# NSA attention operands of 64 and 15 partitions zero-padded to 128, and the first weight slab on ScalarE's queue

## The chip, the cores and the metric

The kernel runs on one core of a Trainium2 chip. The metric is the device time of one execution in microseconds (us), the median of several runs. In the profile PE is TensorE's matmul, PEld its weight load, DVE is VectorE, ACT ScalarE, POOL GpSimd, SP SyncE; SPq is the queue of SyncE that issues DMAs.

## The reference

One hybrid decoder layer on x of 256 tokens and 2048 columns, batch 1, all in float32:

```
xn = rms(x, norm_attn)
fq, fk, fv, f_logit, nq, kc, vc, ks, vs, kw, vw, nsa_gate, gate_a, gate_b = split(xn @ w_in)
o_a = fox_attention(...)                    # 8 heads of 128, causal, with forget gates
o_b = nsa_attention(...)                    # 8 heads, q and k of 192, v of 128, 2 key groups
h = x + (sigmoid(gate_a) * (o_a @ w_up_fox) + sigmoid(gate_b) * (o_b @ w_up_nsa)) @ w_out
y = h + (silu(rms(h) @ w_ffn_gate) * (rms(h) @ w_ffn_up)) @ w_ffn_down
```

The NSA branch adds three attentions under per-head gates: over 15 compressed keys and values (a small MLP over blocks of 32 tokens), over selected blocks, and over a window. With 256 tokens the selection takes every block.

## The kernel before

The kernel is a stream of weight slabs. A `Chunk` is a slab of up to 128 x 1024 float32 weights (two blocks of 128 rows by 512 columns). `load` (L151) issues its DMA from SyncE's queue into one of five `raw` buffers; `split` (L156) makes two parts of it for fp32r matmuls, `hi` on ScalarE (L160) and `lo = raw - hi` on VectorE (L161), four buffers each; `gemm` multiplies them in three passes (L183 high by high, L184 high by low, L185 low by high) for two token tiles of 128, into the PSUM tiles `acc`. The last loop of the program drives the stream: it loads up to eight slabs ahead, splits up to three ahead, issues the matmuls of a slab, and after each calls `slot`, which lets waiting tasks (generators: norms, transposes, attention) go one step on. So the order on every engine is fixed when the program is built, and the attention's matmuls stand between slabs of the weight stream.

At the start of the program SyncE's queue issues `vna` (the gains of the first norm, L119), then the first 512 columns of x for both token tiles (L97), the first two slabs of 512 columns (L153), the next x, and so on. Twelve transposes of the identity (L235) run on TensorE meanwhile. ScalarE starts with a warm activation (L123) that loads its table. VectorE copies the transposed `vna` to `vecT` (L238), clears one column of each key tile (L403), and goes on with the first `lo` (L161) and the low parts of the transposed x (L261).

`nsa_attention` is such a task, and treats eight heads, each in three steps. The score step (L740 to L766) has three blocks of keys of 272, 256 and 272 columns. The 192 columns of a head's q and k are kept as 128 and 64. The first 128 take three passes (L752 to L754). The other 64 are kept twice on 128 partitions: `qb` has the high part of q on partitions 0 to 63 and its low part on 64 to 127, `kbh` the high part of k on both halves, so that L755 does two passes in one matmul. The third pass is L756, high part of q by low part of k, on 64 partitions:

```
nc.tensor.matmul(o, qb[:, h, q], kbh[:, g, k], start=False, stop=False)
nc.tensor.matmul(o, qb[:64, h, q], kbl[:, g, k], start=False, stop=True)
```

`softmax_parts` makes the probabilities on VectorE and ScalarE (L641 to L650). The next step transposes them (L726 to L732) and writes them to `ph`, `pl` and `p1` (L733 to L737); the 15 compressed keys take columns 512 to 767 of `ph` and `pl`, on 15 partitions. The value step (L712 to L716) runs three passes each with `vhl` twice and with `vcg`, the 15 compressed values, on 15 partitions, and then two float32 matmuls with `vsw` (L715, L716), all into one PSUM tile. `put_k` (L375) writes the key tiles, `cmp_finish` (L539) writes `vcg`.

Of the kernel before, what the change touches and what calls it, by code (L numbers as in the profile page):

```python
# [14 lines left out]
P = 128  # L15
# [17 lines left out]
class Chunk:  # L33
    """A slab of weight rows that is loaded, split and multiplied as one unit."""

# [18 lines left out]
def hybrid_block(ctx: ExitStack, tc: tile.TileContext, x, norm_attn, w_in, fox_f_bias,  # L54
# [30 lines left out]
    def wk(shape, tag, bufs, dt=F32):  # L85
        return work.tile(shape, dt, tag=tag, name=nm(tag), bufs=bufs)
# [4 lines left out]

# [1 line left out]
    xin = [u8([P, D]) for _ in range(NT)]  # L93
# [24 lines left out]
    vna = work.tile([16, P], F32, tag="pt", name="vna", bufs=2)  # L118
    nc.sync.dma_start(vna, norm_attn.rearrange("(k p) -> k p", p=P))  # L119
    ident = const.tile([P, P], F32, name="ident")  # L120
    make_identity(nc, ident)
    warm = wk([P, 16], "sm", 12)
    nc.scalar.activation(warm[:, 0:1], ident[:, 0:1], AF.Exp)  # L123

# [1 line left out]
    chunks = []  # L126
# [24 lines left out]
    def load(ch):  # L151
        ch.raw = wpool.tile([P, 1024], F32, tag="raw", name=nm("raw"), bufs=RAW_BUFS)
        nc.sync.dma_start(ch.raw[:, :ch.nkb * ch.n].rearrange("p (k n) -> p k n", k=ch.nkb),  # L153
                          ch.src.rearrange("(k p) n -> p k n", p=P))

# [9 lines left out]
    def gemm(src, c0, n, nkb, stat, done, need=None, sizes=None):  # L165
        """acc[t] = act[t] @ src[:, c0:c0+n]; stat(kb, t, part) is the stationary operand."""
        accs = []
# [31 lines left out]

# [1 line left out]
    vecT = const.tile([P, 46 + 48 + 32], F32, name="vecT")  # L201
# [31 lines left out]
    tp = bank("tp")  # L233
    for _ in range(12):  # keeps the tensor engine awake until the first loads are there
        nc.tensor.transpose(tp[:, 0:P], ident, ident)  # L235
# [11 lines left out]

# [1 line left out]
    def stat_of(tiles):  # L249
        return lambda kb, t, part: tiles[kb // 4][:, part, kb % 4, t * P:(t + 1) * P]  # L250

    def transpose_gain(dst, srcs, q, gcol):
        """columns q*512.. of the two token tiles -> dst[:, hi/lo, 4, 256], times a gain per column."""
        for k in range(4):
            b = bank("tp")[:, :T]
            c = q * 512 + k * P
            for t in range(NT):
                nc.tensor.transpose(b[:, t * P:(t + 1) * P], srcs[t][:, c:c + P], ident)  # L258
            g = vecT[:, gcol + q * 4 + k:gcol + q * 4 + k + 1]
            nc.scalar.activation(dst[:, 0, k], b, AF.Copy, scale=g)  # L260
            nc.vector.scalar_tensor_tensor(dst[:, 1, k], b, g, dst[:, 0, k].bitcast(F32),  # L261
                                           op0=ALU.mult, op1=ALU.subtract)

    def transpose_plain(dst, srcs):
        """two [128, 512] token-major tiles -> dst[:, hi/lo, 4, 256]."""
        for t in range(NT):
# [9 lines left out]
    def rstd_from(dst, ssq, n):  # L276
        """dst = (ssq / n + eps) ** -0.5"""
        w = ssq.shape[-1]
        v = wk([P, 16], "sm", 12)
        nc.vector.tensor_scalar(v[:, :w], ssq, 1.0 / n, EPS, op0=ALU.mult, op1=ALU.add)  # L280
        nc.gpsimd.tensor_tensor(dst, v[:, :w], nhalf[:, :w], op=ALU.pow)  # L281
# [29 lines left out]

# [1 line left out]
    st = {"xa_t": [None] * 3}  # L313

    def head_norm(accs, c0, nh, dk, scale):
        """rms-normalised heads (without gain), token-major: one tile per token tile.
        Heads of width 192 take 256 columns, the last 64 of them a second time."""
        n = NT * nh
# [37 lines left out]
    def nsa_heads_T(qs, nh):  # L356
        """head tiles of one token tile, transposed: [128, h, 128] first part, [64 + 64, h, 128] the rest, twice."""
        b = bank("tp")
# [7 lines left out]
    def put_q(h0, a, b, t):  # L366
        """a kept in float32; the rest as [high; low] parts on the two halves of the partitions."""
        da, db = (st[k][:, h0:h0 + 2, t * P:(t + 1) * P] for k in ("nqa", "nqb"))
# [6 lines left out]
    def put_k(gi, groups, c, n, a, b):  # L375
        """high and low parts; the high part of the rest on both halves of the partitions."""
        ga_, gb_ = vecT[:, VNA + gi:VNA + gi + 1], vecT[:, VNB + gi:VNB + gi + 1]
        ah, al, bh, bl = (k[:, groups, c:c + n] for k in (kah, kal, kbh, kbl))
        nc.scalar.activation(ah, a, AF.Copy, scale=ga_)
# [16 lines left out]

    # key columns of a group: selected 1, selected 0, compressed, window 0, window 1
    kah, kal, kbh = (const.tile([P, 2, 528], F32R, name=n) for n in ("kah", "kal", "kbh"))
    kbl = const.tile([64, 2, 528], F32R, name="kbl")
    zero = const.tile([P, 2], F32, name="zero")  # L400
    nc.gpsimd.memset(zero, 0.0)
    for k in (kah, kal, kbh, kbl):
        nc.vector.tensor_copy(k[:, :, 271], zero[:k.shape[0]])  # L403
    KS, KW = (P, 0), (272, 272 + P)
# [55 lines left out]

# [1 line left out]
    def tok_transpose(y):  # L462
# [72 lines left out]

    vcg = const.tile([15, 2, 2, DV], F32R, name="vcg")

    def cmp_finish(which):
# [20 lines left out]
        if which:  # L559
# [5 lines left out]
            b3 = b[:15, :2 * DV].rearrange("p (g d) -> p g d", g=2)  # L565
            nc.scalar.activation(vcg[:, 0], b3, AF.Copy)
            nc.vector.tensor_tensor(vcg[:, 1], b3, vcg[:, 0].bitcast(F32), op=ALU.subtract)
            return
# [17 lines left out]

# [1 line left out]
    cq = const.tile([P, NT, FH], F32, name="cq")  # L588

    def fox_decay(srcs):  # L590
        """cumulative log-sigmoid: cq[q] token-major and -c[k] broadcast over partitions."""
        z = wk([P, NT, FH], "fd", 8)
# [42 lines left out]
    def softmax_parts(parts, coef):  # L635
        """parts: (scores, bias, out); out = exp(scores + bias - max) * coef / sum, by parts."""
        n = len(parts)
# [18 lines left out]
    def fox_attention():  # L656
# [3 lines left out]
        for s in range(FH + 2):  # L660
# [7 lines left out]
            if 0 <= h < FH:  # L668
                b = bank("tp")
                for j in range(3):  # L670
                    nc.tensor.transpose(b[:, j * P:(j + 1) * P], pb[h][:, j * P:(j + 1) * P], ident)
                pt[h] = wk([P, 1024], "pt", 2)
                nc.vector.tensor_copy(pt[h][:, 0:384], b[:, 0:384])
# [14 lines left out]

# [1 line left out]
    def nsa_attention():  # L690
# [11 lines left out]
        for s in range(NH + 2):  # L702
            h = s - 2
            if h >= 0:
                g = h // 4
                o = bank("O")
                ph, pl, p1 = pt.pop(h)
                for j, (vh, vl, n) in enumerate(((vhl[:, 0, 0, g], vhl[:, 1, 0, g], P),
                                                 (vhl[:, 0, 1, g], vhl[:, 1, 1, g], P),
                                                 (vcg[:, 0, g], vcg[:, 1, g], NCB))):  # L710
                    c = slice(j * T, (j + 1) * T)
                    nc.tensor.matmul(o[:, 0:T], vh, ph[:n, c], start=j == 0, stop=False)  # L712
                    nc.tensor.matmul(o[:, 0:T], vh, pl[:n, c], start=False, stop=False)
                    nc.tensor.matmul(o[:, 0:T], vl, ph[:n, c], start=False, stop=False)
                nc.tensor.matmul(o[:, P:T], vsw[:, 1, 0, g], p1[:, 0:P], start=False, stop=False)  # L715
# [4 lines left out]
            if 0 <= h < NH:  # L720
                ph, pl = (wk([P, 768], "pt", 2, F32R) for _ in range(2))
                p1 = wk([P, T], "qs", 4)
# [7 lines left out]
                for t in range(NT):  # L730
# [3 lines left out]
                nc.vector.tensor_copy(p1, b2[:, 0:T])  # L734
                nc.scalar.activation(ph[:NCB, 512:768], b2[:NCB, T:512], AF.Copy)
                nc.vector.tensor_tensor(pl[:, 0:512], b, ph[:, 0:512].bitcast(F32), op=ALU.subtract)
                nc.vector.tensor_tensor(pl[:NCB, 512:768], b2[:NCB, T:512], ph[:NCB, 512:768].bitcast(F32),  # L737
                                        op=ALU.subtract)
                yield 1
            h = s  # L740
            if h < NH:
# [5 lines left out]
                for c0, n, t in ((0, 272, 1), (272, 256, 1), (P, 272, 0)):  # L747
# [7 lines left out]
                    nc.tensor.matmul(o, qb[:, h, q], kbh[:, g, k], start=False, stop=False)  # L755
                    nc.tensor.matmul(o, qb[:64, h, q], kbl[:, g, k], start=False, stop=True)  # L756
                    sc.append(b)
# [10 lines left out]

# [1 line left out]
    def fox_evac(key, gcol, h0, scale):  # L770
# [60 lines left out]

    # merge gate of the FoX branch, its up projection
    ga = []
# [30 lines left out]

    # NSA branch: gate, up projection, merge
    mT = [None] * 4
# [31 lines left out]

    # output projection and residual
    hs = []  # L900
# [34 lines left out]

# [1 line left out]
    hid = [None] * 11  # L937
# [43 lines left out]

# [1 line left out]
    nload = nsplit = 0  # L983
# [71 lines left out]
```

## Time and profile before

| what | value |
|---|---|
| median of 3 runs | 1480.39 us (1480.22 to 1482.47) |
| span of the profiled execution, first to last instruction | 1478.7 us |
| VectorE busy | 837.5 us (57%) |
| ScalarE busy | 693.5 us (47%) |
| weight loads busy | 1231.7 us (83%) |
| DMA, mean over the span | 188 GB/s |
| granted TensorE clock, mean | 1.000 |

The profiled execution has no time of its own besides its span; the median of the runs lies 1.7 us above it. The busy time of an engine is the time that its instructions cover; that of TensorE counts a matmul from its start to a modelled end, and neighbours overlap. A line of the timeline gives start, duration, engine, line, operation, tiles (out<-in; buffer numbers left out) and count; consecutive instructions of one kind are merged, with the count behind. `128*128` is partitions by columns of the stationary operand, `128x272` the moving one. `m` is a PSUM tile outside the weight stream, `u` and `qs` are working tiles.

### The profile page before, as it was taken

To read this page: it belongs to the slowest core of one execution; us is meant where nothing else is said; L and a number is where in the kernel's file an instruction comes from. 1 tells how busy PE (TensorE), PEld (TensorE's weight loads), DVE (VectorE), ACT (ScalarE), POOL (GpSimd) and SP (SyncE) were. 2 spreads that over 40 slices of the span, in tenths; PEclk is the share of its full clock that TensorE was granted. 3 is DMA by queue.
4 is the path that set the end of the run, shared out by engine and by line. 5 is a ranking of instruction groups with operands and counts; after the bars stand their busy time and mean duration, and the time that the engine had idled before them with its cause. 6 is when DMAs were issued, how large, how long until landed. Compare 5 with 4: busy or idle time off the path is not lost.

```text
span 1478.7 us, 18367 instructions
## 1 busy us (share of the span) xinstructions
PE 1471.8 (100%) x6910; PEld 1231.7 (83%) x6910; DVE 837.5 (57%) x1188; ACT 693.5 (47%) x996; POOL 37.5 (3%) x51
## 2 busy tenths in 40 slices
PE   9999999999999999999999999999999999999998
PEld 7888888998888888888888888888888888888887
DVE  6766766776666555555555554455445455554543
ACT  6465654455556444444454444444333444444432
POOL 2001010010000000000000000000000000000000
PEclk9999999999999999999999999999999999999999
DMA  7577775457332665656656666655556665656562
GB/s 277 176 231 210 253 245 166 133 173 212 116 120 100 195 191 183 196 195 207 211 186 188 189 192 189 191 189 187 195 190 197 190 192 189 186 186 199 200 212 101
DMA packets 151301, 278.70 MB, mean 188 GB/s; under 512 B 9086, under 2 KB 31708, under 8 KB 151084
## 3 DMA queue, kind: packets, MB, share of 16 engines
q1 hardware_dynamic: 150284, 274.04, 58.1%
q0 software_dynamic: 928, 3.48, 0.6%
q8 instruction: 54, 0.88, 0.2%
q14 instruction: 35, 0.29, 0.1%
HBM read 275.38 MB, written 2.11 MB: 188 GB/s over the span
## 4 chain that ended last, share of the span: by engine, by line
PE 99%; DVE 0%; DMA 0%; ACT 0%; issue 0%; POOL 0%; SPq 0%; ACTq 0%; DVEq 0%
PE acc L183 31%; PE acc L185 30%; PE acc L184 30%; PE m L269 1%; PE m L524 1%; PE m L525 1%; PE m L258 1%; PE m L756 1%; PE m L752 0%; PE m L362 0%; PE m L712 0%; DMA u<-in_x_dram 0%; PE m L726 0%; PE m L351 0%; PE m L715 0%; PE m L683 0%
## 5 line engine op out<-in xcount | busy, mean ns | idle before, releaser
L161 DVE TENSOR_TENSOR lo<-raw,hi 128x1024 fp32r<-128x1024 f32 (+4 forms) x525 | 630.3, 1202 | 518.3 <-ACT hi L160 517.5
L160 ACT ACTIVATE hi<-raw 128x1024 fp32r<-128x1024 f32 (+4 forms) x525 | 543.2, 1042 | 557.9 <-PE acc L185 539.3
L183 PE MATMUL acc<-hi,u 128*128 128x512 f32 (+4 forms) x2016 | 787.3, 391 | 0.0
L185 PE MATMUL acc<-hi,u 128*128 128x512 f32 (+4 forms) x2016 | 778.0, 386 | 0.0
L184 PE MATMUL acc<-lo,u 128*128 128x512 f32 (+4 forms) x2016 | 777.6, 386 | 0.4 <-DVE lo L161 0.4
L185 PEld LDWEIGHTS acc<-hi,u 128*128 128x128 f32 x2016 | 378.7, 188 | 74.0
L183 PEld LDWEIGHTS acc<-hi,u 128*128 128x128 f32 x2016 | 378.9, 188 | 71.5 <-ACT u L260 0.3
L184 PEld LDWEIGHTS acc<-lo,u 128*128 128x128 f32 x2016 | 379.1, 188 | 70.8 <-DVE lo L161 0.9
L643 ACT ACTIVATE p<-p,mx 128x256 f32<-128x256 f32 (+2 forms) x64 | 26.3, 411 | 42.0 <-DVE mx L641 42.0
L272 ACT ACTIVATE u<-m 128x512 fp32r<-128x512 f32 x30 | 17.9, 598 | 56.3 <-PE m L269 56.3
L273 DVE TENSOR_TENSOR u<-m,u 128x512 fp32r<-128x512 f32 x30 | 20.8, 692 | 33.3 <-ACT u L272 33.3
L281 POOL TENSOR_TENSOR sm<-sm,nhalf 128x4 f32<-128x4 f32 (+2 forms) x11 | 20.7, 1880 | 262.1 <-DVE sm L280 262.1
L641 DVE CUSTOM_DVE_ANT_0 p<-m,bias 128x256 f32<-128x256 f32 (+2 forms) x64 | 17.5, 309 | 12.1 <-PE m L756 10.8
L323 ACT ACTIVATE qs<-acc,rx 128x128 f32<-128x128 f32 (+1 forms) x56 | 21.0, 398 | 1.6 <-DVE u L395 1.6
L524 PE MATMUL m<-hi,u 128*60 128x256 f32 x80 | 20.0, 284 | 0.0
L945 ACT ACTIVATE qs<-acc,rh 128x512 f32<-128x512 f32 x22 | 15.1, 690 | 9.7 <-PE acc L185 9.7
L525 PE MATMUL m<-lo,u 128*60 128x256 f32 x80 | 19.6, 279 | 0.0
L269 PEld LDWEIGHTS m<-ident,qs 128*128 128x128 f32 x120 | 14.9, 140 | 3.9
L269 PE MATMUL m<-ident,qs 128*128 128x128 f32 x120 | 17.9, 272 | 0.0
L653 ACT ACTIVATE u<-m 128x256 fp32r<-128x256 f32 x16 | 6.1, 379 | 22.2 <-PE m L716 15.0
L958 DVE SCALAR_TENSOR_TENSOR qs<-acc,rh,qs 128x512 f32<-128x512 f32 x22 | 15.4, 743 | 0.0
L650 DVE TENSOR_SCALAR p<-p,mx 128x256 f32<-128x256 f32 (+2 forms) x64 | 14.7, 295 | 0.6
(211 smaller groups left out, 530.4 us busy)
## 6 DMA issues: line engine op xcount, KB each, us to landing
raw<-in_w_in_dram SPq DMA_DIRECT2D x127, 512.0 KB
raw<-in_w_ffn_gate_dram SPq DMA_DIRECT2D x88, 512.0 KB
raw<-in_w_ffn_up_dram SPq DMA_DIRECT2D x88, 512.0 KB
raw<-in_w_ffn_down_dram SPq DMA_DIRECT2D x88, 512.0 KB
raw<-in_w_out_dram SPq DMA_DIRECT2D x32, 512.0 KB
raw<-in_w_in_dram SPq DMA_DIRECT2D x24, 384.0 KB
raw<-in_w_up_fox_dram SPq DMA_DIRECT2D x16, 512.0 KB
raw<-in_w_up_nsa_dram SPq DMA_DIRECT2D x16, 512.0 KB
```

Of the source, the lines that this page charges most:

```text
L160: nc.scalar.activation(hi[:, :m], ch.raw[:, :m], AF.Copy)
L161: nc.vector.tensor_tensor(lo[:, :m], ch.raw[:, :m], hi[:, :m].bitcast(F32), op=ALU.subtract)
L183: nc.tensor.matmul(o, h, ch.hi[:, j], start=first and j == 0, stop=False)
L184: nc.tensor.matmul(o, h, ch.lo[:, j], start=False, stop=False)
L185: nc.tensor.matmul(o, l, ch.hi[:, j], start=False, stop=last and j == w - 1)
L269: nc.tensor.transpose(b[:, j * P:(j + 1) * P], srcs[t][:, j * P:(j + 1) * P], ident)
L273: nc.vector.tensor_tensor(dst[:, 1, :, t * P:(t + 1) * P], b3, hi.bitcast(F32), op=ALU.subtract)
L281: nc.gpsimd.tensor_tensor(dst, v[:, :w], nhalf[:, :w], op=ALU.pow)
L323: nc.scalar.activation(junk[:, :dk], accs[t][:, c0 + j * dk:c0 + (j + 1) * dk], AF.Square, scale=rx[:, t:t + 1], accum_out=ss[:, t * nh + ...
L524: nc.tensor.matmul(o, s, ch.hi[:, j], start=j == 0, stop=False)
L525: nc.tensor.matmul(o, s, ch.lo[:, j], start=False, stop=j == 3)
L643: nc.scalar.activation(o, o, AF.Exp, bias=mx[:, j:j + 1], scale=-1.0, accum_out=sm[:, j:j + 1])
```

## The change

Four edits:

- `kbl` gets 128 partitions; 64 to 127 are set to zero once, and L756 uses all 128 of `qb` and `kbl`. The low part of q on partitions 64 to 127 then meets zeros.
- `vcg` gets 128 partitions, all zero at first, of which 15 are then written. The probabilities of the compressed keys go to `pcT`, two new tiles of 128 partitions, zero at first, taken in turn by heads; 15 partitions are written for each head. The `pt` tiles shrink from 768 (and 1024) columns to 512.
- `zero` becomes a working tile of 128 x 512, cleared on GpSimd; VectorE copies it into the tiles above, in seven copies at the start of its program.
- `vna` and the first slab are issued from ScalarE's queue, and the warm activation comes behind them.

```diff
-    nc.sync.dma_start(vna, norm_attn.rearrange("(k p) -> k p", p=P))
+    nc.scalar.dma_start(vna, norm_attn.rearrange("(k p) -> k p", p=P))
...
-    warm = wk([P, 16], "sm", 12)
-    nc.scalar.activation(warm[:, 0:1], ident[:, 0:1], AF.Exp)
...
-        nc.sync.dma_start(ch.raw[:, :ch.nkb * ch.n].rearrange("p (k n) -> p k n", k=ch.nkb),
-                          ch.src.rearrange("(k p) n -> p k n", p=P))
+        eng = nc.scalar if ch is stream[0] else nc.sync
+        eng.dma_start(ch.raw[:, :ch.nkb * ch.n].rearrange("p (k n) -> p k n", k=ch.nkb),
+                      ch.src.rearrange("(k p) n -> p k n", p=P))
+        if ch is stream[0]:
+            warm = wk([P, 16], "sm", 12)
+            nc.scalar.activation(warm[:, 0:1], ident[:, 0:1], AF.Exp)
...
-        ah, al, bh, bl = (k[:, groups, c:c + n] for k in (kah, kal, kbh, kbl))
+        ah, al, bh, bl = (k[:, groups, c:c + n] for k in (kah, kal, kbh, kbl[0:64]))
...
-    kah, kal, kbh = (const.tile([P, 2, 528], F32R, name=n) for n in ("kah", "kal", "kbh"))
-    kbl = const.tile([64, 2, 528], F32R, name="kbl")
-    zero = const.tile([P, 2], F32, name="zero")
+    kah, kal, kbh, kbl = (const.tile([P, 2, 528], F32R, name=n) for n in ("kah", "kal", "kbh", "kbl"))
+    zero = wk([P, 512], "qs", 4)
     nc.gpsimd.memset(zero, 0.0)
     for k in (kah, kal, kbh, kbl):
-        nc.vector.tensor_copy(k[:, :, 271], zero[:k.shape[0]])
+        nc.vector.tensor_copy(k[:, :, 271], zero[:, 0:2])
+    for g in range(2):
+        nc.vector.tensor_copy(kbl[64:P, g, 0:512], zero[64:P])
+        nc.vector.tensor_copy(kbl[64:P, g, 512:528], zero[64:P, 0:16])
...
-    vcg = const.tile([15, 2, 2, DV], F32R, name="vcg")
+    vcg = const.tile([P, 2, 2, DV], F32R, name="vcg")
+    nc.vector.tensor_copy(vcg.rearrange("p a g d -> p (a g d)"), zero)
+    pcT = [const.tile([P, 2, T], F32R, name=f"pcT{i}") for i in range(2)]
+    for k in pcT:
+        nc.vector.tensor_copy(k.rearrange("p a t -> p (a t)"), zero)
...
-                                                 (vcg[:, 0, g], vcg[:, 1, g], NCB))):
-                    c = slice(j * T, (j + 1) * T)
-                    nc.tensor.matmul(o[:, 0:T], vh, ph[:n, c], start=j == 0, stop=False)
-                    nc.tensor.matmul(o[:, 0:T], vh, pl[:n, c], start=False, stop=False)
-                    nc.tensor.matmul(o[:, 0:T], vl, ph[:n, c], start=False, stop=False)
+                                                    (vcg[:, 0, g], vcg[:, 1, g], pc[:, 0], pc[:, 1]))):
+                    nc.tensor.matmul(o[:, 0:T], vh, a, start=j == 0, stop=False)
+                    nc.tensor.matmul(o[:, 0:T], vh, b, start=False, stop=False)
+                    nc.tensor.matmul(o[:, 0:T], vl, a, start=False, stop=False)
...
-                nc.scalar.activation(ph[:NCB, 512:768], b2[:NCB, T:512], AF.Copy)
+                pc = pcT[h % 2]
+                nc.scalar.activation(pc[:NCB, 0], b2[:NCB, T:512], AF.Copy)
...
-                    nc.tensor.matmul(o, qb[:64, h, q], kbl[:, g, k], start=False, stop=True)
+                    nc.tensor.matmul(o, qb[:, h, q], kbl[:, g, k], start=False, stop=True)
```

TensorE's order does not change; only the operands of these matmuls do. Three queues change at the start of the program. VectorE's, from the copy of `vna`'s gains to the first `lo`, before the change:

```order
L238 COPY vecT<-m_112 128x16
L403 CAST kah<-zero 128x2
L403 CAST kal<-zero 128x2
L403 CAST kbh<-zero 128x2
L403 CAST kbl<-zero 64x2
L161 TENSOR_TENSOR lo_153<-raw_138,hi_152 128x512
```

And after it, from the last of the four small casts on:

```order
L404 CAST kbl<-qs_121 128x2
L406 CAST kbl<-qs_121 64x512
L407 CAST kbl<-qs_121 64x16
L406 CAST kbl<-qs_121 64x512
L407 CAST kbl<-qs_121 64x16
L541 CAST vcg<-qs_121 128x512
L544 CAST pcT_137<-qs_121 128x512
L544 CAST pcT_138<-qs_121 128x512
L163 TENSOR_TENSOR lo_162<-raw_145,hi_161 128x512
```

Seven casts out of the zero tile (a `qs` buffer now) stand ahead of the first `lo`. ScalarE's, from its first instruction on, before:

```order
L123 ACT_TABLE_LOAD
L123 ACTIVATE sm_88<-ident 128x1
L160 ACTIVATE hi_152<-raw_138 128x512
L260 ACTIVATE u_6_115<-m_156,vecT 128x256
L260 ACTIVATE u_6_115<-m_161,vecT 128x256
```

And after the change:

```order
L119 DMA vna<-in_norm_attn_dram 16x128
L152 DMA raw_145<-in_w_in_dram 128x512
L156 ACT_TABLE_LOAD
L156 ACTIVATE sm_147<-ident 128x1
L162 ACTIVATE hi_161<-raw_145 128x512
```

Two DMA issues stand ahead of the table load. SyncE's, from its first DMA on, before (`u` is x):

```order
L119 DMA vna<-in_norm_attn_dram 16x128
L97 DMA u_1_74<-in_x_dram 128x512
L97 DMA u_2_75<-in_x_dram 128x512
L153 DMA raw_138<-in_w_in_dram 128x512
L153 DMA raw_140<-in_w_in_dram 128x512
L97 DMA u_1_74<-in_x_dram 128x512
```

And after:

```order
L97 DMA u_1_74<-in_x_dram 128x512
L97 DMA u_2_75<-in_x_dram 128x512
L152 DMA raw_149<-in_w_in_dram 128x512
L97 DMA u_1_74<-in_x_dram 128x512
L97 DMA u_2_75<-in_x_dram 128x512
```

`vna` and the first slab are gone from it, and every later DMA stands two places further ahead.

## Rows read from the trace of the kernel before

**Rows 1.** Busy time and share of the span by engine, instructions (the page)

```profile
PE 1471.8 (100%) x6910; PEld 1231.7 (83%) x6910; DVE 837.5 (57%) x1188; ACT 693.5 (47%) x996; POOL 37.5 (3%) x51
```

**Rows 2.** What TensorE waited for, whole span: us in total, times, longest

```profile
PE acc L184 <- DVE lo L161: 0.4, 1, 0.4
```

**Rows 3.** Timeline of PE and PEld in one head's score blocks: start us, us, engine, line

```profile
396.62 0.28 PE L754 MATMUL m<-kah,qs 128*128 128x272 f32 x1
396.62 0.19 PEld L755 LDWEIGHTS m<-kbh,u 128*128 128x128 f32 x1
396.74 0.29 PE L755 MATMUL m<-kbh,u 128*128 128x272 f32 x1
396.96 0.18 PEld L756 LDWEIGHTS m<-kbl,u 64*128 64x128 f32 x1
396.96 0.39 PE L756 MATMUL m<-kbl,u 64*128 64x272 f32 x1
397.28 0.39 PE L752 MATMUL m<-kah,qs 128*128 128x256 f32 x1
397.51 0.28 PE L753 MATMUL m<-kal,qs 128*128 128x256 f32 x1
```

**Rows 4.** The same in one head's value step, PE alone

```profile
388.70 0.27 PE L714 MATMUL m<-pt,vhl 128*128 128x256 f32 x1
388.90 0.38 PE L712 MATMUL m<-pt,vcg 15*128 15x256 f32 x1
389.13 0.28 PE L713 MATMUL m<-pt,vcg 15*128 15x256 f32 x1
389.25 0.27 PE L714 MATMUL m<-pt,vcg 15*128 15x256 f32 x1
389.45 0.49 PE L715 MATMUL m<-qs,vsw 128*128 128x128 f32 x2
389.77 0.39 PE L716 MATMUL m<-qs,vsw 128*128 128x128 f32 x2
```

**Rows 5.** The same in a value step of the FoX branch

```profile
303.99 0.33 PE L185 MATMUL acc<-hi,u 128*128 128x384 f32 x1
304.17 0.59 PE L664 MATMUL m<-pt,u 128*128 128x256 f32 x2
304.60 0.38 PE L665 MATMUL m<-pt,u 128*128 128x128 f32 x2
304.82 0.49 PE L671 MATMUL m<-ident,p 128*128 128x128 f32 x3
```

**Rows 6.** All instructions of L756, and of L712 with vcg: min/median/max ns, first and last start

```profile
L756 PE MATMUL m<-kbl,u x24: 380/388/390, 368.1 to 469.2; 64*128 64x272 f32 x16, 64*128 64x256 f32 x8
...
L712 PE MATMUL m<-pt,vcg x8: 382/382/383, 388.9 to 484.1; 15*128 15x256 f32 x8
```

**Rows 7.** Timeline of the start, SP's and ScalarE's queues and VectorE

```profile
0.81 0.39 SPq L119 DMA_DIRECT2D vna<-in_norm_attn_dram  x1
1.26 0.89 SPq L97 DMA_DIRECT2D u<-in_x_dram  x2
2.19 0.91 SPq L153 DMA_DIRECT2D raw<-in_w_in_dram  x2
...
4.80 0.15 DVE L403 CAST kbl<-zero 64x2 fp32r<-64x2 f32 x1
...
6.63 0.63 ACT L160 ACTIVATE hi<-raw 128x512 fp32r<-128x512 f32 x1 [4.33 <-DMA raw<-in_w_in_dram]
...
7.29 0.69 DVE L161 TENSOR_TENSOR lo<-raw,hi 128x512 fp32r<-128x512 f32 x1 [2.34 <-ACT hi L160]
```

**Rows 8.** VectorE's groups by shape: count, busy us, mean ns, idle before

```profile
L650 DVE TENSOR_SCALAR p<-p,mx 128x256 f32<-128x256 f32 x24 | 7.8, 352 | 0.6
...
L469 DVE COPY u<-m 128x512 f32<-128x512 f32 x4 | 2.8, 689 | 2.9 <-PE m L468 2.9
```

**Rows 9.** Busy us of the engines from 400 to 430 us (PE, PEld, DVE, ACT, POOL)

```profile
400.00:430.00 30.00, 30.00 (x155) 24.28 (x154) 18.80 (x64) 17.34 (x49) 0.00 (x0) 1.00 0.36 105
```

More of the change, by code (lines that the diff above doesn't have):

```diff
@@ L565, in cmp_finish @@
             b3 = b[:15, :2 * DV].rearrange("p (g d) -> p g d", g=2)
-            nc.scalar.activation(vcg[:, 0], b3, AF.Copy)
-            nc.vector.tensor_tensor(vcg[:, 1], b3, vcg[:, 0].bitcast(F32), op=ALU.subtract)
+            nc.scalar.activation(vcg[:NCB, 0], b3, AF.Copy)
+            nc.vector.tensor_tensor(vcg[:NCB, 1], b3, vcg[:NCB, 0].bitcast(F32), op=ALU.subtract)
             return
@@ L671, in fox_attention @@
                     nc.tensor.transpose(b[:, j * P:(j + 1) * P], pb[h][:, j * P:(j + 1) * P], ident)
-                pt[h] = wk([P, 1024], "pt", 2)
+                pt[h] = wk([P, 512], "pt", 2)
                 nc.vector.tensor_copy(pt[h][:, 0:384], b[:, 0:384])
@@ L707, in nsa_attention @@
                 ph, pl, p1 = pt.pop(h)
-                for j, (vh, vl, n) in enumerate(((vhl[:, 0, 0, g], vhl[:, 1, 0, g], P),
-                                                 (vhl[:, 0, 1, g], vhl[:, 1, 1, g], P),
-                                                 (vcg[:, 0, g], vcg[:, 1, g], NCB))):
-                    c = slice(j * T, (j + 1) * T)
-                    nc.tensor.matmul(o[:, 0:T], vh, ph[:n, c], start=j == 0, stop=False)
-                    nc.tensor.matmul(o[:, 0:T], vh, pl[:n, c], start=False, stop=False)
-                    nc.tensor.matmul(o[:, 0:T], vl, ph[:n, c], start=False, stop=False)
+                pc = pcT[h % 2]
+                for j, (vh, vl, a, b) in enumerate(((vhl[:, 0, 0, g], vhl[:, 1, 0, g], ph[:, 0:T], pl[:, 0:T]),
+                                                    (vhl[:, 0, 1, g], vhl[:, 1, 1, g], ph[:, T:512], pl[:, T:512]),
+                                                    (vcg[:, 0, g], vcg[:, 1, g], pc[:, 0], pc[:, 1]))):
+                    nc.tensor.matmul(o[:, 0:T], vh, a, start=j == 0, stop=False)
+                    nc.tensor.matmul(o[:, 0:T], vh, b, start=False, stop=False)
+                    nc.tensor.matmul(o[:, 0:T], vl, a, start=False, stop=False)
                 nc.tensor.matmul(o[:, P:T], vsw[:, 1, 0, g], p1[:, 0:P], start=False, stop=False)
@@ L720, in nsa_attention @@
             if 0 <= h < NH:
-                ph, pl = (wk([P, 768], "pt", 2, F32R) for _ in range(2))
+                ph, pl = (wk([P, 512], "pt", 2, F32R) for _ in range(2))
                 p1 = wk([P, T], "qs", 4)
@@ L734, in nsa_attention @@
                 nc.vector.tensor_copy(p1, b2[:, 0:T])
-                nc.scalar.activation(ph[:NCB, 512:768], b2[:NCB, T:512], AF.Copy)
+                pc = pcT[h % 2]
+                nc.scalar.activation(pc[:NCB, 0], b2[:NCB, T:512], AF.Copy)
                 nc.vector.tensor_tensor(pl[:, 0:512], b, ph[:, 0:512].bitcast(F32), op=ALU.subtract)
-                nc.vector.tensor_tensor(pl[:NCB, 512:768], b2[:NCB, T:512], ph[:NCB, 512:768].bitcast(F32),
-                                        op=ALU.subtract)
+                nc.vector.tensor_tensor(pc[:NCB, 1], b2[:NCB, T:512], pc[:NCB, 0].bitcast(F32), op=ALU.subtract)
                 yield 1
```

## The prediction

> **What bounds the kernel now.** I read the busy shares first, then what TensorE waited for, then the order in time around the lines that the change touches. TensorE is busy for 1471.8 of 1478.7 us [rows 1], and the largest wait that another engine's arithmetic causes it is one of 0.4 us for a low part of the weights [rows 2]; most of the rest lies in the first microseconds, when loads are still coming, and behind its last matmul. So whatever makes TensorE's own row of instructions shorter makes the program shorter. A busy TensorE need not be streaming, though: a matmul's recorded time overlaps its successor's, so what it costs is the distance from its start to the next start. That distance is what I read below.
>
> In the score block of a head (L752 to L756) the undisturbed distance for 272 columns is 0.12 us: L754 at 396.62, L755 at 396.74. L756 is the one matmul with 64 partitions (64*128). It starts 0.22 after L755; L752 of the next group starts 0.32 after it; and L753 starts 0.23 after that L752, where a matmul of 256 columns otherwise takes 0.12 [rows 3, 4]. The reason stands in the loads: the load for L755 begins at 396.62, together with the matmul before it, but the load for L756 begins only at 396.96, long after L755's start, with its matmul [rows 3]. The weights of a 64-partition matmul are not loaded behind a 128-partition one, nor the reverse. The third L756 of a head is followed by the weight stream's L183 in place of L752; I count its exit like the other two.
>
> The value step shows the same with 15 partitions: L712 with vcg starts 0.20 after L714 (0.12 is usual), L713 0.23 after it, L714 0.12 after that, and on the way back L715 0.20 after L714, with 0.32 for the L715 pair [rows 4]. An undisturbed pair of the same shape, L665, takes 0.22 [rows 5]; records come in pairs for a float32 matmul. There are 24 L756 and 8 of these vcg triples [rows 6].
>
> **The change, part by part.**
>
> *kbl and the left side of L756 padded to 128.* The columns stay the same, so streaming costs the same. What goes is the excess: 0.22 - 0.12 on entry, 0.32 - 0.12 on exit, 0.23 - 0.12 on the matmul behind it: 0.10 + 0.20 + 0.11 = 0.41 us, times 24 = 9.8 us.
>
> *vcg and pcT padded to 128.* (0.20 - 0.12) + (0.23 - 0.12) + (0.20 - 0.12) + (0.32 - 0.22) = 0.37 us, times 8 = 3.0 us. Together 12.8 us. Starts are given to 0.01 us, and I take 0.6 us either way for that.
>
> The price that padding could have is bounded by rows too. The load is no longer than any other: neighbours of 128 partitions load in 0.19 us, L756's in 0.18 [rows 3]. If a padded load could be hidden like its neighbours' it costs nothing; if it had to wait as L752's does after L756, its matmul would start 0.32 after the one before. I take the first value, since it is what each row between two 128-partition matmuls shows; the second is a rival below.
>
> *What stands beside TensorE.* The 12.8 us lie between 368 and 484 us [rows 6]. There VectorE was busy 18.80 and ScalarE 17.34 of 30 us [rows 9]; with 11% taken from the stretch they would stand at about 70% and 65%, so neither becomes the bound. The writes into vcg and pcT keep their shapes of 15 rows. pcT exists twice and alternates by head, as the two pt buffers did, so there is no new wait for a free buffer. After the stretch TensorE is still the one that is waited for, so the gain should reach the end whole.
>
> *Seven zero fills on VectorE.* They stand after the four casts that end at 4.95 and ahead of the first low part (L161 at 7.29), in a gap in which VectorE had 2.34 us idle [rows 7]. Five have 512 columns, two have 16. The nearest rows for 512 columns from SBUF are 0.352 us for L650's 256 columns, one source in SBUF, and 0.689 us for L469's 512 columns out of PSUM [rows 8]. A fill reads SBUF, as L650 does, so I go nearer to that row and take 0.45; five of these and 0.15 for each small one make 2.55 us, and the fills end at about 7.5, 0.2 us late for the first low part. The bounds are 5 x 0.35 = 1.75 us (end 6.7, nothing late) and 5 x 0.69 + 0.3 = 3.75 us (end 8.7, 1.4 us late). [...] The memset on GpSimd that they read grows from 2 to 512 columns; it is covered as long as it is done when VectorE comes to the casts, the last of which began at 4.80 [rows 7].
>
> *vna and the first slab on ScalarE's queue, the warm activation behind them.* SP gave vna 0.39 us of issue and each slab about 0.45 [rows 7]. Without them x is issued 0.45 us sooner, and all later slabs 0.9 sooner. The first slab, issued at about 2.2, was there at 6.63, when ScalarE stopped waiting for it; ScalarE's queue can issue it at about 1.2. It then shares the DMA engines with the first x columns, whose issue ended at 2.15 [rows 7]. ScalarE itself had waited 4.33 us there, so two issues and the table load cost it nothing. All in all I expect the stream to settle 0.3 us sooner: most of the 0.4 us wait for the low part [rows 2] goes, as the loads come earlier, and the rest of the relief is held up by VectorE's fills. Bounds: 0.9 us sooner (all of SP's relief arrives) and 1.1 us later (fills at the slow price, less the 0.3 us of that wait which then is covered).
>
> **Sum.** 1478.7 - 12.8 - 0.3 = 1465.6 us of span. The median of the runs, 1480.4, lies 1.7 us above that span, and I leave this distance as it is: 1467.3 us. With the bounds above, 1466 to 1469.
>
> **The rivals.**
>
> *Only part of it goes.* The exit from vcg leads into L715, a float32 matmul, so some of that bubble may belong to the change of type; or a softmax step that had a few us in hand comes late when its neighbours move closer. If only kbl's part goes: 1480.4 - 9.8 - 0.3 = 1470.3; half of all, 1473.7. Against it: L664, float32 too, starts 0.18 after the weight stream's L185 [rows 5] with nothing added for the change of type, and the first L712 with vcg pays the same 0.08 without one. Chance 0.10.
>
> *The bubble has another cause and stays.* It might come with the end of a group in a PSUM bank, or with kbl as an operand. Then the time is that of the start alone, 1480.1. Against it: vcg's bubble is in the middle of its accumulation, and the two share nothing but the number of partitions. Chance 0.06.
>
> *Slower: padded loads wait.* If weights of 128 partitions that follow a 128-partition matmul cannot be loaded during it, because both use all rows of the array, then L756 would start 0.32 after L755 instead of 0.22, and the three vcg matmuls 0.32 after their predecessors instead of 0.20, 0.23 and 0.12: 24 x 0.10 + 8 x 0.41 = 5.7 us more, and 1485.8. It decides if a 128-partition load does not begin before the matmul ahead of it has ended. The rows speak against it: the load for L755 begins at the start of L754 [rows 3]. [...] Chance 0.04.
>
> **How the numbers follow.** The forecast has 0.80. About 0.2%, 3 us, is what a measurement of this kernel can tell from no change. The forecast and the partial case are both faster by more: 0.90; the bubble that stays is within it: 0.06; slower 0.04. The range takes the forecast's own bounds, a spread of the median of 1 us below and 2 above (the three runs lay between 1480.22 and 1482.47), and the case of kbl alone: 1465.0 to 1471.5.
>
> **What would show it.** Right: L756 shown as 128*128 and starting 0.12 after L755, L752 0.12 after it, the vcg triple at 0.12 each, and a median of L756 near 290 ns instead of 388; the stretch of the eight heads some 12.8 us shorter, and TensorE with no idle in it. The fills: seven casts between 5 and 7.5 us, and the first L161 no later than 7.6. The first hi before 6.63. Wrong: distances of 0.2 to 0.3 that stay around the padded matmuls, a new wait of TensorE on L650 or L737 in the heads, or a first L161 after 8 us.

## The result and the profile after

| | median | runs |
|---|---|---|
| before | 1480.63 us | 1480.22 to 1482.47, 5 runs |
| changed | 1467.61 us | 1466.92 to 1468.69, 5 runs |

The ratio is 0.9909, 95% interval 0.9897 to 0.9921: 13.0 us faster, where 1467.3 us and 13.1 us less than the then median had been forecast. The profiled execution's span went from 1478.7 to 1465.9 us. The page of the changed kernel:

```profile
PE 1458.4 (99%) x6910; PEld 1227.8 (84%) x6910; DVE 838.8 (57%) x1195; ACT 692.4 (47%) x996; POOL 37.9 (3%) x51
```

TensorE is busy 13.4 us less, as against [rows 1], with the same number of matmuls. VectorE is where it was, with the seven fills added. What TensorE still waited for in the whole span, in the form of [rows 2]:

```profile
PE m L237 <- POOL nhalf L211: 1.4, 1, 1.4
PE m L260 <- DMA u<-in_x_dram: 1.3, 2, 1.1
PE acc L186 <- DVE lo L163: 0.4, 1, 0.4
PE acc L185 <- ACT u L262: 0.3, 1, 0.3
```

The waits for GpSimd, for x and for L262 lie in the first 8 us. That for a low part is of the same 0.4 us as in [rows 2]; in both traces it lies at 306 us, ahead of the heads. There is no wait in the heads, neither on a softmax step nor on the writes to pcT. The score block of one head, as in [rows 3] (lines have moved; L762 to L764 and L760 to L761 are the former L754 to L756 and L752 to L753):

```profile
394.05 0.29 PE L762 MATMUL m<-kah,qs 128*128 128x272 f32 x1
394.18 0.19 PEld L764 LDWEIGHTS m<-kbl,u 128*128 128x128 f32 x1
394.18 0.29 PE L763 MATMUL m<-kbh,u 128*128 128x272 f32 x1
394.31 0.29 PE L764 MATMUL m<-kbl,u 128*128 128x272 f32 x1
394.43 0.29 PE L760 MATMUL m<-kah,qs 128*128 128x256 f32 x1
394.55 0.28 PE L761 MATMUL m<-kal,qs 128*128 128x256 f32 x1
```

Each matmul starts 0.12 to 0.13 us after the one before, through the padded L764 and out of it. The load for L764 begins at 394.18, together with L763's matmul; in [rows 3] the load for L756 began 0.22 after L755. The value step, as in [rows 4]:

```profile
386.54 0.28 PE L722 MATMUL m<-pt,vhl 128*128 128x256 f32 x1
386.65 0.28 PE L720 MATMUL m<-pcT,vcg 128*128 128x256 f32 x1
386.78 0.28 PE L721 MATMUL m<-pcT,vcg 128*128 128x256 f32 x1
386.89 0.28 PE L722 MATMUL m<-pcT,vcg 128*128 128x256 f32 x1
387.01 0.38 PE L723 MATMUL m<-qs,vsw 128*128 128x128 f32 x2
387.23 0.39 PE L724 MATMUL m<-qs,vsw 128*128 128x128 f32 x2
```

The vcg triple has distances of 0.13, 0.11 and 0.12, L723 starts 0.12 after it, and its pair takes 0.22, as the undisturbed pair in [rows 5] does. All 24 padded matmuls, as in [rows 6]:

```profile
L764 PE MATMUL m<-kbl,u x24: 280/288/293, 368.2 to 457.8; 128*128 128x272 f32 x16, 128*128 128x256 f32 x8
```

The recorded time of one fell from 388 to 288 ns. It overlaps its neighbours and is not the gain; the distances are.

To separate the heads from the rest I use two starts in each trace: the first score matmul of the first head, and the first weight matmul behind the value step of the last. What lies between is called the heads.

| kernel | first score matmul | behind the heads | heads | against before |
|---|---|---|---|---|
| before | 367.48 | 485.15 | 117.67 | |
| changed | 367.65 | 472.72 | 105.07 | -12.60 |
| e1, kbl only | 368.90 | 477.21 | 108.31 | -9.36 |
| e2, vcg only | 368.74 | 483.10 | 114.36 | -3.31 |
| e3, queue only | 367.19 | 484.86 | 117.67 | 0.00 |
| e4, 65 partitions | 367.99 | 473.36 | 105.37 | -12.30 |
| e5, padding without queue | 367.61 | 472.69 | 105.08 | -12.59 |
| e6, narrow ones side by side | 367.58 | 482.05 | 114.47 | -3.20 |
| e7, narrow ones spread | 368.17 | 492.13 | 123.96 | +6.29 |
| e8, transposes padded too | 366.90 | 471.97 | 105.07 | -12.60 |

So of the 12.8 us by which the changed kernel's span is shorter, 12.60 come from the heads; the stretch before them is 0.17 longer, and the one behind them 0.35 shorter.

### The profile page after: what moved, and what is told of

The parts are those of the page before. It is cut to its first block, busy times and chain, and to the rows that moved or that the text cites. A ratio compares the mean times of both kernels' runs of the same rounds, so it can differ in the third digit from the quotient of the medians.

```text
span 1465.9 us, 18375 instructions
## 1 busy us (share of the span) xinstructions
PE 1458.4 (99%) x6910; PEld 1227.8 (84%) x6910; DVE 838.8 (57%) x1195; ACT 692.4 (47%) x996; POOL 37.9 (3%) x51
## 4 chain that ended last, share of the span: by engine, by line
PE 98%; DVE 0%; DMA 0%; ACT 0%; issue 0%; POOL 0%; SPq 0%; ACTq 0%; DVEq 0%
PE acc L185 31%; PE acc L187 31%; PE acc L186 31%; PE m L271 1%; PE m L528 1%; PE m L529 1%; PE m L260 1%; PE m L364 0%; DMA u<-in_x_dram 0%; PE m L734 0%; PE m L353 0%; PE m L691 0%; PE m L764 0%; PE m L760 0%; PE m L761 0%; PE m L763 0%
## 5 line engine op out<-in xcount | busy, mean ns | idle before, releaser
L185 PE MATMUL acc<-hi,u 128*128 128x512 f32 (+4 forms) x2016 | 786.0, 390 | 0.3 <-ACT u L262 0.3
L187 PE MATMUL acc<-hi,u 128*128 128x512 f32 (+4 forms) x2016 | 777.8, 386 | 0.0
L187 PEld LDWEIGHTS acc<-hi,u 128*128 128x128 f32 x2016 | 378.7, 188 | 73.8 <-DVE u L263 0.2
L185 PEld LDWEIGHTS acc<-hi,u 128*128 128x128 f32 x2016 | 378.8, 188 | 70.2 <-ACT u L262 0.6
L529 PE MATMUL m<-lo,u 128*60 128x256 f32 x80 | 19.6, 279 | 0.0
L974 DVE TENSOR_TENSOR u<-acc,u 128x512 f32<-128x512 f32 x16 | 10.4, 683 | 7.9 <-PE acc L187 7.9
```

Of the source, the lines that this page charges most:

```text
L185: nc.tensor.matmul(o, h, ch.hi[:, j], start=first and j == 0, stop=False)
L187: nc.tensor.matmul(o, l, ch.hi[:, j], start=False, stop=last and j == w - 1)
L529: nc.tensor.matmul(o, s, ch.lo[:, j], start=False, stop=j == 3)
```

## Experiments

**One part at a time.** Four kernels, measured beside the kernel before (1481.07 us). In e1 only these edits are made, with `zero` at 512 columns and four of the fills:

```diff
+    kah, kal, kbh, kbl = (const.tile([P, 2, 528], F32R, name=n) for n in ("kah", "kal", "kbh", "kbl"))
...
-                    nc.tensor.matmul(o, qb[:64, h, q], kbl[:, g, k], start=False, stop=True)
+                    nc.tensor.matmul(o, qb[:, h, q], kbl[:, g, k], start=False, stop=True)
```

> Only kbl and the left side of L756 are padded; vcg and the queues are as before. Theory (each passage between a matmul of 128 partitions and one of fewer costs about 0.2 us, and 48 of the 64 passages are at L756): the heads are 9.5 to 9.8 us shorter, time 1470.5 to 1471.5 us. Rival (kbl's part is a matter of a few us, and vcg or the queues carry the gain): 1475 or more.

Measured: 1471.86 us, ratio 0.9936 (0.9923 to 0.9950). The heads are 9.36 us shorter, 0.39 for each L756, where 0.41 had been read from one block of one head. Both figures lie a little outside what was expected, the heads by 0.14 us and the median by 0.36; the rival, 1475 or more, is refuted.

In e2 it is the other part: vcg and pcT of 128 partitions, three fills, kbl and queues as before.

```diff
+    vcg = const.tile([P, 2, 2, DV], F32R, name="vcg")
...
+                                                    (vcg[:, 0, g], vcg[:, 1, g], pc[:, 0], pc[:, 1]))):
```

> Only vcg and the probabilities of the compressed keys are padded; kbl and the queues are as before. Theory: 16 passages go, 3.0 to 3.1 us, time 1477.3 to 1477.9 us. Rival (the exit into the float32 L715 is slow for its type): the distances from L714 to L715 and in the L715 pair stay at 0.20 and 0.32, 1.5 us go, time near 1479.

Measured: 1477.49 us, ratio 0.9977 (0.9968 to 0.9985); the heads 3.31 us shorter. The exit into the float32 L715 had been slow for the passage, not for its type: in e2 that matmul starts 0.12 after the last vcg one (472.04 and 472.16), and its pair takes 0.22. Together e1 and e2 give 9.36 + 3.31 = 12.67 us, and both edits at once 12.60: the parts add up.

In e3 there is no padding and no fill, only the queue edit.

```diff
-    nc.sync.dma_start(vna, norm_attn.rearrange("(k p) -> k p", p=P))
+    nc.scalar.dma_start(vna, norm_attn.rearrange("(k p) -> k p", p=P))
...
+        eng = nc.scalar if ch is stream[0] else nc.sync
```

> Only the queue edit: vna and the first slab from ScalarE's queue, the warm activation behind them, no padding and no fills. Theory: within 0.5 us of the kernel before (1480.1 to 1480.9), since the first x and the first slab share the DMA engines whatever queue issues them. Rival (without the fills on VectorE the queue's relief of 0.9 us arrives): 1479.7 or less.

Measured: 1480.47 us, ratio 0.9995 (0.9987 to 1.0004). It can't be told from no change; in its profile the first score matmul starts 0.29 sooner than before.

In e5 both paddings and all seven fills are there, and `vna` and the first slab stay on SyncE's queue.

```diff
-        eng = nc.scalar if ch is stream[0] else nc.sync
-        eng.dma_start(ch.raw[:, :ch.nkb * ch.n].rearrange("p (k n) -> p k n", k=ch.nkb),
+        nc.sync.dma_start(ch.raw[:, :ch.nkb * ch.n].rearrange("p (k n) -> p k n", k=ch.nkb),
```

> Both paddings and all seven fills, the queues as before. Theory: all of the gain but what the queue gives, 1467.3 to 1468.2 us. Rival (the fills hold up the first low part, and the queue edit pays for it): 1468.5 or more, with the first low part on VectorE well after 7.3 us.

Measured: 1467.93 us, ratio 0.9913 (0.9900 to 0.9927), the same span as the changed kernel's, 1465.9. The first low part began at 7.65 us, as soon as the high part was there; the fills had ended 0.61 us before. The queue edit contributes nothing that these runs can tell from zero.

**What exactly costs.** Three kernels, again measured beside the kernel before (1480.96 us). e4 asks how many partitions are enough:

```diff
-                    nc.tensor.matmul(o, qb[:, h, q], kbl[:, g, k], start=False, stop=True)
+                    nc.tensor.matmul(o, qb[:65, h, q], kbl[:65, g, k], start=False, stop=True)
...
-                                                    (vcg[:, 0, g], vcg[:, 1, g], pc[:, 0], pc[:, 1]))):
+                                                    (vcg[:65, 0, g], vcg[:65, 1, g], pc[:65, 0], pc[:65, 1]))):
```

> The changed kernel, but L764 and the vcg triple use 65 of the 128 partitions. Theory (the array has a setting for up to 64 partitions, and passages between it and the full one cost; 65 are already in the full one): same as the changed kernel, 1467 to 1468.5 us, distances of 0.12. Rival (any partition count that differs from the neighbour's costs): the distances of 0.2 and 0.3 come back, 1480 us.

Measured: 1467.99 us, ratio 0.9910 (0.9894 to 0.9927). The timeline of a score block of e4:

```profile
368.37 0.29 PE L763 MATMUL m<-kbh,u 128*128 128x272 f32 x1
368.50 0.29 PE L764 MATMUL m<-kbl,u 65*128 65x272 f32 x1
368.62 0.28 PE L760 MATMUL m<-kah,qs 128*128 128x256 f32 x1
368.75 0.28 PE L761 MATMUL m<-kal,qs 128*128 128x256 f32 x1
```

The shape is 65*128 and the distances are 0.13, 0.12 and 0.13. It is not the full 128 that counts here, and not equality with the neighbour: 65 partitions, one more than the 64 of before, are enough.

e6 leaves the narrow matmuls as they were and changes only who stands beside whom:

```diff
+                    mid = c0 == 272
+                    if mid:
+                        nc.tensor.matmul(o, qb[:64, h, q], kbl[:, g, k], start=True, stop=False)
...
-                    nc.tensor.matmul(o, qb[:64, h, q], kbl[:, g, k], start=False, stop=True)
+                    if not mid:
+                        nc.tensor.matmul(o, qb[:64, h, q], kbl[:, g, k], start=False, stop=True)
```

> The kernel before, with L756 moved to the front of the middle block, so that two of a head's three 64-partition matmuls stand side by side; the same matmuls in number and shape. Theory (passages cost, not narrow matmuls): 4 passages per head instead of 6, 16 fewer in all at 0.2 us, 3.1 us less, 1477.2 to 1477.8. Rival (each narrow matmul is slow by itself): no change, 1480.3 to 1480.9.

Measured: 1478.55 us, ratio 0.9982 (0.9973 to 0.9991); the heads 3.20 us shorter, which is 0.20 for each of the 16 passages taken away. The median is 0.75 us above the expected range; in the profiled execution, which took 1477.44 us, the heads are shorter as forecast (3.1 us). The timeline of one head of e6, from the last full matmul before the pair:

```profile
396.07 0.29 PE L758 MATMUL m<-kbh,u 128*128 128x272 f32 x1
396.28 0.39 PE L760 MATMUL m<-kbl,u 64*128 64x272 f32 x1
396.51 0.28 PE L754 MATMUL m<-kbl,u 64*128 64x256 f32 x1
396.72 0.39 PE L755 MATMUL m<-kah,qs 128*128 128x256 f32 x1
396.94 0.28 PE L756 MATMUL m<-kal,qs 128*128 128x256 f32 x1
```

Each passage shows twice. The first narrow matmul starts 0.21 after L758, and the second 0.23 after the first, where 0.12 to 0.13 are usual; then the same on the way back, 0.21 and 0.22. So a passage costs about 0.09 us ahead of the first matmul of the new kind and about 0.11 behind it. The next one starts at 397.06, 0.12 later again.

e7 goes the other way, and puts each vcg matmul between vhl ones:

```diff
+                for i, (j, m) in enumerate(((0, 0), (0, 1), (2, 0), (0, 2), (1, 0), (2, 1), (1, 1), (1, 2), (2, 2))):
```

> The kernel before, with the three vcg matmuls of 15 partitions spread among the six vhl ones instead of in a row; the same matmuls in number and shape. Theory: 6 passages per head instead of 2, 32 more at 0.2 us, 6.2 us more, 1486 to 1487.5. Rival (each narrow matmul is slow by itself): no change, 1480.3 to 1480.9.

Measured: 1487.91 us, ratio 1.0046 (1.0031 to 1.0061); the heads 6.29 us longer, 0.197 for each of the 32 passages added. The median is 0.4 us above the expected range, the heads are within what was expected. In its timeline the pairs of vhl matmuls and the single vcg ones take turns:

```profile
388.80 0.40 PE L713 MATMUL m<-pt,vhl 128*128 128x256 f32 x2
389.12 0.38 PE L713 MATMUL m<-pt,vcg 15*128 15x256 f32 x1
389.44 0.50 PE L713 MATMUL m<-pt,vhl 128*128 128x256 f32 x2
389.87 0.38 PE L713 MATMUL m<-pt,vcg 15*128 15x256 f32 x1
```

A vcg matmul and its passage take 0.32 us, the pair of full ones behind it 0.43 where two undisturbed distances would be 0.24.

**Further in the same direction.** e8 is the changed kernel with the small transposes padded as well: the gains of the norms (46, 16 and 32 partitions), the hidden layer of the compression (60) and its keys (30). For instance:

```diff
-        nc.tensor.transpose(b[:, 0:30], kn[:30, 0:P], ident[:30, :30])
-        nc.tensor.transpose(b[:, 32:62], kn[:30, P:2 * P], ident[:30, :30])
+        nc.tensor.transpose(b[:, 0:P], kn[:, 0:P], ident)
+        nc.tensor.transpose(b[:, P:2 * P], kn[:, P:2 * P], ident)
```

> The changed kernel, and also the transposes of 46, 16, 32, 60 and 30 partitions (L244 to L247, L550, L591 and L592) padded with zeros to 128. Theory (any passage between the full array and fewer partitions costs, for transposes too): some 8 passages at 0.2 us go, 1.6 us, and eleven transposes get wider at up to 0.06 us each, 0.6 us: 0.7 to 1.2 us less between the first weight matmuls and the heads, 1466.4 to 1467.0 us. Rival (transposes don't pay for passages, or the rest of that distance is a wait): no change or 0.6 us more there, 1467.6 to 1468.2.

Measured: 1467.01 us, ratio to before (1481.39 us) 0.9903 (0.9886 to 0.9919). The interval is wider than the step from the changed kernel, but the trace shows the step. From the first weight matmul behind the second lot of transposes of x (11.47 in e8, 11.49 in the changed kernel) to the first score matmul it is 355.43 us instead of 356.16, 0.73 less; in the other nine profiles this distance lies between 356.15 and 356.78. The gain falls where the padded transposes stand: counted from matmul to matmul, 0.16 to 0.24 us at each of their four groups (28, 177, 193 and 231 us), and under 0.04 us the other way in every stretch between. The two transposes of the compressed keys, in the changed kernel:

```profile
192.36 0.39 PE L187 MATMUL acc<-hi,u 128*128 128x512 f32 x1
192.68 0.24 PE L591 MATMUL m<-ident,qs 30*128 30x30 f32 x1
192.76 0.22 PE L592 MATMUL m<-ident,qs 30*128 30x30 f32 x1
192.91 0.33 PE L528 MATMUL m<-hi,u 128*60 128x256 f32 x1
193.08 0.28 PE L529 MATMUL m<-lo,u 128*60 128x256 f32 x1
```

And in e8:

```profile
191.97 0.39 PE L187 MATMUL acc<-hi,u 128*128 128x512 f32 x1
192.20 0.27 PE L595 MATMUL m<-ident,qs 128*128 128x128 f32 x1
192.31 0.27 PE L596 MATMUL m<-ident,qs 128*128 128x128 f32 x1
192.34 0.36 PE L531 MATMUL m<-hi,u 128*60 128x256 f32 x1
192.54 0.28 PE L532 MATMUL m<-lo,u 128*60 128x256 f32 x1
```

From L187 to L529, the second matmul behind the transposes (L532 in e8), it took 0.72 us, and now 0.57, although each transpose is wider. This version has the lowest median of all; it is ahead of the changed kernel by 0.6 us, which the medians alone don't settle.

## Why the prediction was right

**The bubble.** The main term was 9.8 + 3.0 = 12.8 us; the heads became 12.60 us shorter, and e1 and e2 put 9.36 and 3.31 on the two parts. That is 12.60 / 64 = 0.197 us for each passage, 16 of the 64 at vcg and 48 at L756, the same price as e6 and e7 show with the shapes left alone. It came out well because it was read from starts. By the recorded times the sum would have been 24 times 0.10 us, since 388 ns fell to 288. What lies behind each passage, the late next load, shows only in the distance to the next start but one. [rows 3] has the late load on the way into L756. On the way back, in the same block of the kernel before, the load for L752 is late too: it begins with its own matmul, 0.32 after L756's start:

```profile
397.28 0.19 PEld L752 LDWEIGHTS m<-kah,qs 128*128 128x128 f32 x1
```

That the total missed by only 0.3 us is in part luck. The heads gave 0.2 us less than forecast and the start 0.47 less, and 0.35 us that nobody had forecast came behind the heads.

**Rivals.** That padded loads wait is refuted by the load for L764: in the changed kernel it begins at 394.18, with the matmul ahead of it. Loads of 128 partitions run there beside matmuls of 128; it is where 64 partitions meet 128 that the load was late (396.96 and 397.28, in the kernel before). That both use all rows of the array, as that rival supposes, no run shows, nor a setting of the array, of which the expectation of e4 speaks; what the runs show is that 65 partitions behave as 128 (e4, distances of 0.12 to 0.13 us), and that 64 and 15 pay much the same for a passage, 9.36 / 48 = 0.195 us and 3.31 / 16 = 0.207 us (e1, e2). What TensorE does in that time no trace here shows; shown is the late load and the 0.197 us. The rival by which only a part goes is refuted by e2 and by heads in which TensorE has no wait, the one by which the bubble has another cause by e4, e6 and e7.

**What stands beside TensorE.** The shares of 70% and 65% forecast for the shorter stretch were borne out: VectorE was busy 71.65 and ScalarE 64.53 of 100 us (columns as in [rows 9]).

```profile
372.00:472.00 100.00, 100.00 (x568) 87.07 (x567) 71.65 (x220) 64.53 (x152) 0.00 (x0) 1.00 0.42 127
```

**The start.** Here the prediction failed in a small term: the stream was to settle 0.3 us sooner because most of the 0.4 us wait for a low part [rows 2] would go, and in the changed kernel's profile the first score matmul starts 0.17 later. The step itself was misread: [rows 2] gives that wait for the whole span, and I placed it at the start. It lies between 300 and 360 us, in a slab of 384 columns, and is still there after the change; loads that come earlier at the start have nothing to do with it. Nor is that wait the largest on another engine's arithmetic, as the prediction has it: [rows 2] is short of the 1.4 us that TensorE waits for GpSimd ahead of the identity's transposes, before the change as behind it. That wait is over at 1.43 us and does not touch the argument. The start of the changed kernel, as in [rows 7], with TensorE's transposes of x (L260):

```profile
0.81 0.86 SPq L97 DMA_DIRECT2D u<-in_x_dram  x2
1.25 0.44 ACTq L152 DMA_DIRECT2D raw<-in_w_in_dram  x1
...
5.00 0.42 DVE L406 CAST kbl<-qs 64x512 fp32r<-64x512 f32 x1
...
6.14 0.98 PE L260 MATMUL m<-ident,u 128*128 128x128 f32 x7 [1.13 <-DMA u<-in_x_dram]
6.28 0.76 DVE L544 CAST pcT<-qs 128x512 fp32r<-128x512 f32 x2
6.41 0.63 ACT L162 ACTIVATE hi<-raw 128x512 fp32r<-128x512 f32 x1 [3.19 <-DMA raw<-in_w_in_dram]
...
7.07 0.69 DVE L163 TENSOR_TENSOR lo<-raw,hi 128x512 fp32r<-128x512 f32 x1
...
10.09 1.65 PE L260 MATMUL m<-ident,u 128*128 128x128 f32 x8
...
11.49 0.48 PE L185 MATMUL acc<-hi,u 128*128 128x512 f32 x1
```

The fills were sized well: from 5.00 to 7.04 us, 2.04 instead of 2.55; one of 512 columns takes 0.42 and the next starts 0.34 after it. In this profile they end when the high part does, both at 7.04, so it can't say which of the two the first low part (7.07) waited for. In e5 the fills end at 7.04 too and the slab came later, and there the low part begins 0.03 us after the high part's end, at 7.65: the fills were not what held it up.

The first slab was issued at 1.25 instead of about 2.2, and was there at 6.41 instead of 6.63. That difference can't be put down to the queue: over the ten profiles the slab is there between 6.40 (e6) and 7.17 us (e1) with the queues of the kernel before, and between 6.39 (e3) and 7.17 (e4) with the new ones. What the queue edit did move is x. The first transpose of x waits for it until 4.64 and 4.68 with the new queues (e3 and the changed kernel) and until 4.81 to 4.97 with the old (the kernel before, e1, e2 and e5); the next seven wait for their part until 6.01 and 6.14, as against 5.68 to 5.98. So of the 0.45 us by which x is issued sooner the first part keeps some, and the second comes later than it did. That fits loads which share the DMA engines: in the first 8 us of the changed kernel the packets of two queues, q1 and q10, took 57.6% and 11.4% of the time of the 16 engines, and these were busy for 0.93 of the stretch from 4 to 5 us and 1.01 from 5 to 6 (0.90 and 0.93 in the kernel before, all on q1). Whether there one load loses what another gains was not tried apart.

The largest step at the start falls where the granted clock was low. In the changed kernel the eight transposes that begin at 10.09 are followed by L185 at 11.49, 1.40 later. In the kernel before it was 0.79:

```profile
10.20 1.04 PE L258 MATMUL m<-ident,u 128*128 128x128 f32 x8
10.99 0.49 PE L183 MATMUL acc<-hi,u 128*128 128x512 f32 x1
```

And in e3, with the same queues as the changed kernel, it was 0.80 (10.07 to 10.87).

The granted clock of the changed kernel's profile in these stretches (the column before the DMA share) was 0.50 and then 0.67, the mean of 0.50 up to 11.3 us and 1.00 behind it:

```profile
8.00:10.00 2.00, 2.00 (x5) 1.42 (x6) 1.93 (x5) 1.25 (x4) 0.00 (x0) 0.50 1.05 405
10.00:12.00 2.00, 2.00 (x11) 1.87 (x10) 1.15 (x2) 2.00 (x5) 0.00 (x0) 0.67 0.97 318
```

At 0.50 its 512-column matmuls start 0.43 us apart (8.80 to 10.09), and 0.23 at 1.00 (from 11.81 on). TensorE had waited 1.13 us for loads until 6.14, and then 0.33 ahead of L185 at 7.45. From 4.6 to 7.9 us the profile gives 1.00, and the seven transposes at 6.14 took 0.98, where the kernel before took 1.75 for them; so by this profile the clock had been up, fell and rose once more. What makes it fall or rise no run shows. A step as long comes without the change too, as in e7, whose start is that of the kernel before: with the old queues, the eight transposes and the way to the next weight matmul took 1.56 us in e1, e2 and e7, whose profiles give 1.00 from 0 to 14 us, and 0.79 in the kernel before, e5 and e6; with the new queues it was 0.80 (e3), 0.90 (e4, whose profile gives 0.50 for 8 to 10 us and 0.71 for 10 to 12), 0.93 (e8) and 1.40. Of the 0.50 us by which the changed kernel is behind at 11.49, 0.33 is made up before the first score matmul, and the causes of that were not traced. Over the ten profiles the first score matmul starts between 366.90 and 368.90; a term of 0.3 us is far below what the start does by itself from one execution to the next.

**Behind the heads** the changed kernel is 0.35 us faster over 993 us, in small steps along the whole stretch. e1, e2, e4, e5 and e8, which all have the zero tile among the `qs` buffers, show 0.3 to 0.4 us as well, and e3, e6 and e7, which don't, 0.0. The cause was not tried and stays open.

## What to carry to other kernels

Where a stream of full matmuls on TensorE contains a few with fewer partitions than the rest (64 and 15 here), count the passages between the two kinds, not the narrow matmuls; each passage cost 0.2 us here. Zeros up to 128 partitions, or up to 65 (e4), removed it, and the padded matmuls started 0.11 to 0.13 us apart like their neighbours; where that can't be done, narrow ones put side by side share their passages (e6, 0.20 us for each of the 16 saved). Read such a cost from start to start, including the matmul behind it: a busy share of 100% hid 12.6 us of it.

## What was not expected

- 65 partitions are as good as 128: distances of 0.12 to 0.13 us in e4, and heads within 0.3 us of the fully padded ones (105.37 and 105.07).
- Transposes pay for the passage too: from L187 past two of them it is 0.72 us with 30 partitions and 0.57 with 128 (e8).
- In the kernel before, the profile gives a granted clock of 1.00 for 8 to 10 us (the columns are those of the changed kernel's rows above):

```profile
8.00:10.00 2.00, 2.00 (x6) 1.57 (x6) 2.00 (x5) 1.24 (x3) 0.00 (x0) 1.00 1.04 395
```

But the 512-column matmuls there start 0.42 to 0.43 us apart, as against 0.43 in the changed kernel's stretch at 0.50; later it is 0.23. So in this profile the recorded clock and the distances do not agree at the start. From these distances I estimate that the record is not complete there; no run shows it.
